# Modulation columns by block transposes and a sum along the free axis, in place of products with a column of ones

## The chip, the cores and the metric

The kernel runs on one core of one Trainium2 chip. The metric is the device time of one execution in microseconds (us). A core has a matrix engine (TensorE, PE in the profile, with its weight loads as PEld), a vector engine (VectorE, DVE), an activation engine (ScalarE, ACT), GpSimd (POOL), and a sync engine (SyncE, SP) whose queue here issues the loads from HBM. TensorE writes to PSUM, eight banks of 128 partitions x 512 fp32 numbers; the other engines read PSUM and SBUF.

## The reference

Two layers of a diffusion backbone: 256 latent tokens with 256 context tokens, 1024 features. Layer 0 is latent attention with a gated linear recurrence beside it, layer 1 a Hyena operator; each layer ends in a mixture of 16 experts. What the change touches is the modulation: a vector of 1024 conditioning features is multiplied with a 1024 x 6144 matrix per layer, and its six pieces of 1024 shift, scale or gate the activations.

```python
mod = (silu_c @ ada_w[layer] + ada_b[layer])[:, None, :]
sh1, sc1, g1, sh2, sc2, g2 = jnp.split(mod, 6, axis=-1)
h_lat = modulate(rms_norm(x, norm1_g[layer]), sh1, sc1)     # h * (1 + sc1) + sh1
...
x = x + g1 * o_lat
h_lat = modulate(rms_norm(x, norm2_g[layer]), sh2, sc2)
```

For the context tokens of layer 0 the same is done with a second conditioning vector. All is fp32.

## The kernel before

The matrix `ada_w` is used once, as a vector times a matrix, so it is streamed from HBM in tiles of 1 MB through a ring of nine buffers (the name `w`), in one fixed order of loads on SyncE's queue that the other weights share. A piece of 1024 outputs, called step (l, s), is made in two halves of 512. Pieces 0 and 1 of layer 0 are made in the prologue (`ada_first`). The later ones are made in the background of other work: `ada_step` does one of eight portions of a step each time it is called. A table (`PLAN`) says by which engine each half is made.

- A "V" half: VectorE multiplies each row of weights with its conditioning scalar and adds, lines 444 and 446. The result `e` is 128 x 512, a partial sum in each partition, and the sum over the 128 partitions is still to be made.
- A "P" half: TensorE multiplies with the conditioning columns `cs`, 32 wide, four products side by side in the four 32-column groups of the array, line 437, and ScalarE copies the result out. In `e` there are then four partial sums, in partitions 0, 32, 64 and 96, and everything between them is zero.

A step that is done ripens for a few calls (`LAG`). Then a gate piece is spread over rows (`ada_row`), and a shift or scale piece is turned into columns of 128 features by `ada_columns`: it takes the 512 numbers of a half to four columns of 128 partitions. It does this with a product: a block of 128 x 128 of `e` is the stationary operand and a column of ones (or, in the prologue, two columns of zeros and ones, `selc`, one for the latent and one for the context vector) is the moving one, so that the sum over partitions comes out with the features along the partitions. VectorE then adds the bias out of PSUM (line 377), and for a scale piece takes 1 + scale times the gain of the norm (line 379).

`ada_columns` is called 16 times: four times in the prologue (pieces 0 and 1 of layer 0, two halves, both vectors), and 12 times later in pairs, one pair for each of the steps (0,3), (0,4), (1,0), (1,1), (1,3) and (1,4). Step (0,3) has two V halves, (1,4) two P halves, the other four one of each.

What lies around the late calls: the recurrence (lines 898 to 925), the key, value and query projections (lines 953 to 1013), and attention by heads: scores (line 1078) with the row maxima on VectorE (lines 1079 and 1080) and the exponential on ScalarE (line 1081); the 128 x 128 transposes of the probabilities (line 1091); their products with the values, 64 columns wide (line 1105), scaled by VectorE (line 1108); and a transpose of these (line 1114). Then comes the output projection (`project_out`, line 512), and layer 0's experts (from line 1199 on). Tables of numbers (`SEQ`, `ATT`, `OUTB`) say how many background portions are put in at which place. Each engine works through its own queue in order. The build arranges every queue by its own estimate of when operands are there, so that rows of several lines are mixed, and a change in one function moves others.

Of the kernel before, what the change touches and what calls it, by code (L numbers as in the profile page):

```python
# [14 lines left out]
OP = mybir.AluOpType  # L15
# [46 lines left out]
PLAN = {(0, 3): "VV", (1, 2): "VV", (1, 4): "PP", (1, 5): "PP"}  # L62
# [104 lines left out]
def build(tc, A, dbg=None, stop=None):  # L167
    nc = tc.nc
    V, S, G, T = nc.vector, nc.scalar, nc.gpsimd, nc.tensor
# [18 lines left out]
    def ps():  # L188
        return pp.tile([128, 512], F32, tag="ps", name=nm("ps"))
# [138 lines left out]
    ident = kc[:, KC["ident"]:KC["ident"] + 128]  # L328
    tri = kc[:, KC["tri"]:KC["tri"] + 128]
    selrow = kc[:, KC["selrow"]:KC["selrow"] + 128]  # L330
    selc = kc[:, KC["selc"]:KC["selc"] + 2]
    iota = kc[:, KC["iota"]:KC["iota"] + CAP]
    lt = kc[:, KC["lt"]:KC["lt"] + 16]
    ones = kp.tile([128, 128], F32, name="ones")
# [30 lines left out]

    grow = {}

    def ada_columns(l, s, hf, use, e, lcol, n):
        p2 = ps()
        for m in range(4):  # L370
            T.matmul(p2[:, n * m:n * m + n], e[:, m * 128:m * 128 + 128], lcol[:, :n], start=True, stop=True)
        pv = p2[:, :4 * n].rearrange("p (m n) -> p m n", n=n)
        b = pc("adab", l * 48 + s * 8 + hf * 4, 4)
        for i in range(n):
            kind = ("c" if i else "") + ("1" if s < 3 else "2")
            o = mc(l, use + kind)[:, hf * 4:hf * 4 + 4]
            V.tensor_tensor(o, pv[:, :, i], b, op=OP.add)
            if use == "sc":
                V.scalar_tensor_tensor(o, o, 1.0, pc("n1" if s < 3 else "n2", l * 8 + hf * 4, 4),
                                       op0=OP.add, op1=OP.mult)  # L380
# [28 lines left out]
    def ada_step():  # L409
        for r in ripe:  # L410
            r[0] += 1
        if ripe and ripe[0][0] > LAG:
            l, s, use, e = ripe.pop(0)[1]
            for hf in range(2):
                if use == "row":
                    r = l * 12 + s * 2 + hf
                    V.scalar_tensor_tensor(e[hf][0:24], adab, ident[0:24, r:r + 1], e[hf][0:24], op0=OP.mult, op1=OP.add)
                    ada_row(l, s, hf, e[hf])
                else:
                    ada_columns(l, s, hf, use, e[hf], ones, 1)  # L420
        if not current:
            if not todo:
                return bool(ripe)
            e = ada_alloc[0]("e", 2, 512)
# [34 lines left out]
    def bg(n=1):  # L459
        for _ in range(n):  # L460
            ada_step()
# [300 lines left out]
    with ExitStack() as pa:  # L762
# [22 lines left out]
        for i, (src, dst) in enumerate(((ctx, ctxn), (x, y))):  # L785
            for k2 in range(4):
                p = ps()
                for k in (2 * k2, 2 * k2 + 1):
                    for t in range(2):
                        m = k % 2 * 256 + t * 128  # L790
# [42 lines left out]
        for hf in range(2):  # L833
            e = []
            for s in range(2):
                if hf and not UXL:
                    ux_sum(2 * s, 0)
                    if s == 0:
                        ux_sum(1, 0)
                e.append(ada_first(s, hf, t4))  # L840
            for s, use in enumerate(("sh", "sc")):
                ada_columns(0, s, hf, use, e[s], selc, 2)
            if hf and not UXL:
                ux_sum(3, 0)
            for k in range(4 * hf, 4 * hf + 4):
                for i, (o, kd) in enumerate(((0, "c1"), (256, "1"))):
                    v = hT[hf][:, k % 4, o:o + NT]
                    m, a = mc(0, "sc" + kd)[:, k:k + 1], mc(0, "sh" + kd)[:, k:k + 1]
                    if (2 * k + i) % 3:
                        V.tensor_scalar(v, v, m, a, op0=OP.mult, op1=OP.add)  # L850
                    else:
                        S.activation(v, v, AF.Identity, scale=m, bias=a)
# [290 lines left out]
    n = NW + N8 - 3 + NX[0]  # L1143
# [371 lines left out]
    with w0 as ws:  # L1515
# [14 lines left out]
        r = moe(0, route0, ws, filters, FJ, FILLS, turned)  # L1530
# [6 lines left out]
        p = ps()  # L1537
        for t in range(2):
            o = slice(t * 128, t * 128 + 128)
# [228 lines left out]
```

## Time and profile before

| what | us |
| --- | --- |
| median of 3 runs | 955.71 |
| lowest and highest of them | 954.07, 956.16 |
| the profiled execution's own time | 955.92 |
| its span in the trace | 954.1 |
| TensorE busy in the span | 874.8 |
| VectorE busy in the span | 458.9 |
| ScalarE busy in the span | 228.6 |

The profile comes from one execution, so durations and sums belong to its 955.92 us; the span is the part between the first and the last instruction in the trace. An engine's busy time says what share of the span it worked, not whether the end waits for it; the waits, and the timeline of the stretch, say that. In timelines, a row is a run of equal instructions: its start, its length from the first to the end of the last, the count, and in brackets how long the engine sat idle before it and what ended that. A fp32 product shows as two records, one for each of its passes; a transpose shows as one.

### The profile page before, as it was taken

The numbers are of one execution on the slowest core, as the hardware profiler recorded it, in microseconds if no ns is written. First come the engines' busy times: TensorE is split into PE (matmuls) and PEld (weight loads), VectorE is DVE, ScalarE is ACT, GpSimd is POOL, SyncE is SP. The second block draws the span as 40 slices with busy tenths as digits, with TensorE's granted clock in tenths as the row PEclk, the third lists the DMA queues.
The fourth block names the chain that finished last, engine by engine and source line by source line (L and its number), as shares of the span: only waits on it lengthen the run. The fifth ranks groups of instructions, "written<-read, shape, count | busy, mean of one in ns | idle before, by whom it ended". The sixth has DMA issues, their size and how long they took to land. (4 is left out here: it accounts for less than half of the span.)

```text
span 954.1 us, 10948 instructions
## 1 busy us (share of the span) xinstructions
PE 874.8 (92%) x4040; PEld 457.0 (48%) x4040; DVE 458.9 (48%) x1104; ACT 228.6 (24%) x446; POOL 15.7 (2%) x21
## 2 busy tenths in 40 slices
PE   3998999999989999899999599999999999988984
PEld 2444755575553543333443288677554442322421
DVE  5359775762464464445522466876172333122123
ACT  3266413440321122222211312211031110100112
POOL 0000000000000010101100000000000000000000
PEclk9999999998989999999999799999989999999997
DMA  9956679476499999999989883642289999999994
GB/s 350 344 186 242 226 242 356 159 258 221 166 371 393 369 337 387 388 397 396 393 331 347 308 276 121 242 155 89 89 298 396 390 396 387 403 390 397 397 386 151
DMA packets 130567, 289.32 MB, mean 303 GB/s; under 512 B 6828, under 2 KB 8876, under 8 KB 130500
## 3 DMA queue, kind: packets, MB, share of 16 engines
q1 hardware_dynamic: 129428, 286.39, 82.2%
q10 hardware_dynamic: 1072, 2.10, 0.7%
q8 instruction: 35, 0.57, 0.2%
q14 instruction: 32, 0.26, 0.1%
HBM read 287.42 MB, written 1.05 MB: 302 GB/s over the span
## 5 line engine op out<-in xcount | busy, mean ns | idle before, releaser
L1239 PE MATMUL ps<-w,xe 128*64 128x512 f32 (+1 forms) x696 | 173.5, 597 | 2.6 <-DMA w<-in_moe_w 2.6
L1239 PEld LDWEIGHTS ps<-w,xe 128*64 128x64 f32 (+1 forms) x696 | 49.9, 129 | 87.8 <-issue 79.1
L1267 PE MATMUL ps<-w,at 128*64 128x512 f32 (+1 forms) x344 | 86.0, 597 | 4.5 <-DMA w<-in_moe_w 2.7
L1589 PE MATMUL ps<-xt,w 128*128 128x256 f32 x384 | 87.6, 388 | 1.8 <-ACT xt L1553 1.8
L1589 PEld LDWEIGHTS ps<-xt,w 128*128 128x128 f32 x384 | 74.6, 196 | 14.4 <-ACT xt L1553 2.1
L1286 DVE TENSOR_TENSOR x<-x,ps 128x512 f32<-128x512 f32 x56 | 37.0, 684 | 62.5 <-PE ps L1284 62.5
L1273 DVE SCALAR_TENSOR_TENSOR ye<-ps,gs,grow 128x512 f32<-128x512 f32 x28 | 21.0, 748 | 85.1 <-PE ps L1267 85.1
L1239 PE MATMUL ps<-sp,xe 128*64 128x512 f32 (+1 forms) x216 | 54.8, 598 | 1.4 <-DMA sp<-in_moe_w 1.4
L446 DVE SCALAR_TENSOR_TENSOR e<-w,sg,e 128x512 f32<-128x512 f32 x70 | 51.5, 746 | 3.5 <-DMA w<-in_ada_w 2.8
L1267 PEld LDWEIGHTS ps<-w,at 128*64 128x64 f32 (+1 forms) x344 | 26.8, 130 | 50.5 <-issue 39.8
L1275 ACT ACTIVATE yeh<-ye 128x512 fp32r<-128x512 f32 x28 | 17.6, 630 | 119.6 <-DVE ye L1273 119.6
L1239 PE MATMUL ps<-x,xe 128*64 128x512 f32 (+1 forms) x112 | 37.5, 596 | 1.6 <-DMA x<-in_moe_w 1.6
L1249 DVE TENSOR_TENSOR th<-th,ps 128x512 f32<-128x512 f32 x14 | 9.6, 688 | 59.8 <-PE ps L1239 59.8
L1239 PEld LDWEIGHTS ps<-sp,xe 128*64 128x64 f32 (+1 forms) x216 | 16.0, 132 | 30.2 <-issue 26.8
L1267 PE MATMUL ps<-sp,at 128*64 128x512 f32 (+1 forms) x112 | 27.4, 599 | 3.0 <-ACT at L345 1.7
L1215 ACT ACTIVATE xe<-ps,modc 128x256 f32<-128x256 f32 (+1 forms) x32 | 15.8, 539 | 59.8 <-DVE xe L1213 59.8
L830 PE MATMUL ps<-hT,w 128*128 128x512 f32 x64 | 29.7, 623 | 0.4 <-DMA w<-in_ev_w_in 0.4
L512 PE MATMUL ps<-w,x 128*128 128x512 f32 x64 | 28.4, 595 | 0.7 <-ACT x L1603 0.7
L512 PE MATMUL ps<-w,mix 128*128 128x512 f32 x64 | 28.9, 603 | 0.0
L1244 ACT ACTIVATE th<-ps 128x512 f32<-128x512 f32 x14 | 8.4, 597 | 82.3 <-PE ps L1239 66.8
L1277 DVE TENSOR_TENSOR yel<-ye,yeh 128x512 fp32r<-128x512 f32 x28 | 19.3, 691 | 16.7 <-ACT yeh L1275 10.4
L437 PE MATMUL ps<-w,cs 128*32 128x512 f32 x160 | 27.3, 689 | 0.0
(355 smaller groups left out, 1334.2 us busy)
## 6 DMA issues: line engine op xcount, KB each, us to landing
w<-in_moe_w SPq DMA_DIRECT2D x126, 1024.0 KB, 14.0
w<-in_ada_w SPq DMA_DIRECT2D x48, 1024.0 KB, 7.2
sp<-in_moe_w SPq DMA_DIRECT2D x41, 1024.0 KB, 14.9
x<-in_moe_w SPq DMA_DIRECT2D x21, 1024.0 KB, 14.1
w<-in_od_w_in SPq DMA_DIRECT2D x12, 1024.0 KB, 8.0
w<-in_ev_w_in SPq DMA_DIRECT2D x4, 1024.0 KB, 10.9
w<-in_ev_w_out SPq DMA_DIRECT2D x4, 1024.0 KB, 7.3
w<-in_moe_w SPq DMA_DIRECT2D x8, 512.0 KB, 9.8
```

Of the source, the lines that this page charges most:

```text
L437: T.matmul(part[hf][32 * q:32 * q + 32, :], cs[:, k - 3 + q, :], get(("ada", l, s, hf, k // 4))[:, q, :], start=(k == 3), stop=(k == 7), t ...
L446: V.scalar_tensor_tensor(eh, w[hf], c, eh, op0=OP.mult, op1=OP.add)
L512: T.matmul(po[t][n], a[:, k, t * 128:t * 128 + 128], b[:, n * 512:n * 512 + 512], start=(k == korder[0] and i == 0), stop=(k == korder[-1] ...
L830: T.matmul(uxp[b], get(("wux", hf))[:, k % 4, b * 128:b * 128 + 128], hT[hf][:, k % 4, :], start=(k == 0), stop=(k == KD - 1))
L1215: S.activation(e[:, k, :w], p[:, w:2 * w], AF.Identity, scale=sc[:, k:k + 1], bias=sh[:, k:k + 1])
L1239: T.matmul(p[room * i:room * i + room, :], xe[j // 2][:, k, o:o + room], weight(nme, e, k), start=(k == 0), stop=(k == KD - 1), tile_posit ...
L1267: T.matmul(p[room * i:room * i + room, :], act[j][:, o:o + room], weight("w2", e, k, n), start=(k == 0), stop=(k == 3), tile_position=(0, ...
L1273: V.scalar_tensor_tensor(e, po[j, n], gs[j], grow[l, 5][:, n * 512:n * 512 + 512], op0=OP.mult, op1=OP.mult)
L1275: S.activation(h, e, AF.Copy)
L1277: V.tensor_tensor(o, e, h.bitcast(F32), op=OP.subtract)
L1286: V.tensor_tensor(xs, xs, p, op=OP.add)
L1589: T.matmul(pb, w[:, k % 4, b * 128:b * 128 + 128], hT[:, k, :], start=(k == 0 and b % 2 == 0), stop=(k == KD - 1 and b % 2 == 1))
```

## The change

`ada_columns` makes the four blocks into transposes (out of `e` into the four quarters of a whole PSUM bank) and lets VectorE sum along the free axis, which now holds what were the partitions. Of a V half (and of nothing else) all 128 numbers of a row are summed, 128 partitions x 4 x 128; of a P half and in the prologue only the four that are not zero, strided by 32 (`four`). The bias is then added from SBUF to SBUF. The prologue's calls make two such short sums, one for each vector. In all there are 64 transposes where there were 64 products, and 20 reductions more on VectorE: 6 full ones and 14 short ones, 8 of these in the prologue. Behind the function all line numbers are 5 higher.

```diff
--- before.py
+++ after.py
@@ -365,16 +365,21 @@
 
     grow = {}
 
-    def ada_columns(l, s, hf, use, e, lcol, n):
+    def ada_columns(l, s, hf, use, e, four, n):
+
         p2 = ps()
         for m in range(4):
-            T.matmul(p2[:, n * m:n * m + n], e[:, m * 128:m * 128 + 128], lcol[:, :n], start=True, stop=True)
-        pv = p2[:, :4 * n].rearrange("p (m n) -> p m n", n=n)
+            T.transpose(p2[:, m * 128:m * 128 + 128], e[:, m * 128:m * 128 + 128], ident)
+        pv = p2.rearrange("p (m q r) -> p m q r", m=4, q=4)
         b = pc("adab", l * 48 + s * 8 + hf * 4, 4)
         for i in range(n):
             kind = ("c" if i else "") + ("1" if s < 3 else "2")
             o = mc(l, use + kind)[:, hf * 4:hf * 4 + 4]
-            V.tensor_tensor(o, pv[:, :, i], b, op=OP.add)
+            if four:
+                V.tensor_reduce(o, pv[:, :, :, i], axis=mybir.AxisListType.X, op=OP.add)
+            else:
+                V.tensor_reduce(o, p2.rearrange("p (m r) -> p m r", m=4), axis=mybir.AxisListType.X, op=OP.add)
+            V.tensor_tensor(o, o, b, op=OP.add)
             if use == "sc":
                 V.scalar_tensor_tensor(o, o, 1.0, pc("n1" if s < 3 else "n2", l * 8 + hf * 4, 4),
                                        op0=OP.add, op1=OP.mult)
@@ -417,7 +422,7 @@
                     V.scalar_tensor_tensor(e[hf][0:24], adab, ident[0:24, r:r + 1], e[hf][0:24], op0=OP.mult, op1=OP.add)
                     ada_row(l, s, hf, e[hf])
                 else:
-                    ada_columns(l, s, hf, use, e[hf], ones, 1)
+                    ada_columns(l, s, hf, use, e[hf], PLAN.get((l, s), "VP")[hf] == "P", 1)
         if not current:
             if not todo:
                 return bool(ripe)
@@ -839,7 +844,7 @@
                         ux_sum(1, 0)
                 e.append(ada_first(s, hf, t4))
             for s, use in enumerate(("sh", "sc")):
-                ada_columns(0, s, hf, use, e[s], selc, 2)
+                ada_columns(0, s, hf, use, e[s], True, 2)
             if hf and not UXL:
                 ux_sum(3, 0)
             for k in range(4 * hf, 4 * hf + 4):
```

The order on the engines moves too. TensorE at attention, where step (1,0) becomes columns (`e_1071` before, `e_1083` after); the order of before, then that of after, in which line 372 is the transpose, 442 was 437, 1083 was 1078, 1096 was 1091 and 1119 was 1114:

```order
L371 MATMUL ps_1265<-ones,e_1071 128x1 x4
L371 MATMUL ps_1271<-ones,e_1071 128x1 x4
L437 MATMUL ps_1278<-w_1215,cs 32x512 x4
L1078 MATMUL ps_1284<-kT_948,qT_949 128x512
L1078 MATMUL ps_1289<-kT_948,qT_949 128x512
L1114 MATMUL ps_1294<-kc,o_1248 128x128 x2
L1091 MATMUL ps_1299<-kc,pm_1218 128x128 x4
L437 MATMUL ps_1278<-w_1313,cs 32x512 x2
L1091 MATMUL ps_1305<-kc,pm_1218 128x128 x4
L1078 MATMUL ps_1317<-kT_948,qT_949 128x512
L1078 MATMUL ps_1322<-kT_948,qT_949 128x512
L437 MATMUL ps_1278<-w_1313,cs 32x512 x2
```

```order
L372 MATMUL ps_1277<-kc,e_1083 128x128 x4
L372 MATMUL ps_1284<-kc,e_1083 128x128 x4
L442 MATMUL ps_1292<-w_1227,cs 32x512 x4
L1083 MATMUL ps_1298<-kT_960,qT_961 128x512
L1083 MATMUL ps_1303<-kT_960,qT_961 128x512
L442 MATMUL ps_1292<-w_1327,cs 32x512 x4
L1119 MATMUL ps_1308<-kc,o_1260 128x128 x2
L1096 MATMUL ps_1313<-kc,pm_1230 128x128 x4
L1096 MATMUL ps_1319<-kc,pm_1230 128x128 x4
L1083 MATMUL ps_1331<-kT_960,qT_961 128x512
L1083 MATMUL ps_1336<-kT_960,qT_961 128x512
```

The four packed products of the second weight tile stood two and two, around transposes and scores; now they stand together.

TensorE a little later, where step (1,1) becomes columns (`e_1204` before, `e_1216` after) between the products of the probabilities with the values (`vt` and `pt`); the order of before, then of after, in which line 1110 was 1105 and 442 was 437:

```order
L1105 MATMUL ps_1393<-vt_698,pt_1348 128x64 x2
L371 MATMUL ps_1415<-ones,e_1204 128x1 x4
L371 MATMUL ps_1422<-ones,e_1204 128x1 x3
L1105 MATMUL ps_1393<-vt_698,pt_1348 128x64 x6
L1105 MATMUL ps_1393<-vt_698,pt_1367 128x64 x8
L371 MATMUL ps_1422<-ones,e_1204 128x1
L437 MATMUL ps_1430<-w_1389,cs 32x512 x4
L437 MATMUL ps_1430<-w_1437,cs 32x512 x4
L1114 MATMUL ps_1442<-kc,o_1412 128x128 x2
```

```order
L1110 MATMUL ps_1407<-vt_708,pt_1362 128x64 x2
L372 MATMUL ps_1429<-kc,e_1216 128x128 x4
L372 MATMUL ps_1437<-kc,e_1216 128x128 x4
L442 MATMUL ps_1446<-w_1403,cs 32x512 x4
L1110 MATMUL ps_1407<-vt_708,pt_1362 128x64 x6
L1110 MATMUL ps_1407<-vt_708,pt_1381 128x64 x8
L442 MATMUL ps_1446<-w_1453,cs 32x512 x4
L1119 MATMUL ps_1458<-kc,o_1426 128x128 x2
```

The last product of the columns no longer stands behind the block of value products, and the packed products of the first weight tile moved from behind that block to ahead of it.

VectorE at the first of these places, from the columns' bias add on; before, then after, in which 381 is the full reduction, 379 the short one, 382 the bias add and 1084 was 1079:

```order
L377 TENSOR_TENSOR modc<-ps_1265,pk 128x4
L446 SCALAR_TENSOR_TENSOR e_1204<-w_1311,sg,e_1204 128x512
L377 TENSOR_TENSOR modc<-ps_1271,pk 128x4
L1079 TENSOR_REDUCE nmx<-ps_1284 128x1
L1080 TENSOR_SCALAR nmx<-nmx 128x1
L1079 TENSOR_REDUCE nmx<-ps_1289 128x1
L1080 TENSOR_SCALAR nmx<-nmx 128x1
L343 COPY pt_1298<-ps_1305 128x512
```

```order
L381 TENSOR_REDUCE modc<-ps_1277 128x4
L451 SCALAR_TENSOR_TENSOR e_1216<-w_1325,sg,e_1216 128x512
L379 TENSOR_REDUCE modc<-ps_1284 128x4
L382 TENSOR_TENSOR modc<-modc,pk 128x4
L1084 TENSOR_REDUCE nmx<-ps_1298 128x1
L382 TENSOR_TENSOR modc<-modc,pk 128x4
L1085 TENSOR_SCALAR nmx<-nmx 128x1
L1084 TENSOR_REDUCE nmx<-ps_1303 128x1
L1085 TENSOR_SCALAR nmx<-nmx 128x1
L343 COPY pt_1312<-ps_1319 128x512
```

Two reductions are new, and they and the bias adds stand ahead of the row maximum of the next scores, or between it and its scaling.

## Rows read from the trace of the kernel before

**Rows 1.** The page: the span, the engines' busy time, the granted clock by slices.
```profile
span 954.1 us, 10948 instructions
PE 874.8 (92%) x4040; PEld 457.0 (48%) x4040; DVE 458.9 (48%) x1104; ACT 228.6 (24%) x446; POOL 15.7 (2%) x21
...
PEclk9999999998989999999999799999989999999997
```

**Rows 2.** The chain that ended last, its earliest piece: start us, us, what.
```profile
542.60 0.09 issue
```

**Rows 3.** Waits of TensorE, 100 to 232 us: in total, times, longest us.
```profile
PE ps L1091 <- ACT pm L1081: 1.2, 1, 1.2
```

**Rows 4.** Waits of SyncE's load queue, 140 to 280 us, the first.
```profile
SPq L219 <- PE ps L512: 30.8, 4, 13.4
```

**Rows 5.** Instructions of line 371: ns min/median/max, first and last start, forms.
```profile
L371 PEld LDWEIGHTS ps<-ones,e x96: 188/192/334, 102.2 to 276.1; 128*128 128x128 f32 x96
L371 PE MATMUL ps<-ones,e x96: 167/251/353, 102.5 to 276.2; 128*128 128x1 f32 x96
```

**Rows 6.** Timeline at pairs A (first row) and C: start us, us.
```profile
102.23 2.00 PEld L371 LDWEIGHTS ps<-ones,e 128*128 128x128 f32 x16
...
197.60 1.86 PEld L371 LDWEIGHTS ps<-ones,e 128*128 128x128 f32 x16
...
199.48 1.07 PE L437 MATMUL ps<-w,cs 128*32 128x512 f32 x8
...
203.05 1.05 PE L437 MATMUL ps<-w,cs 128*32 128x512 f32 x4
```

**Rows 7.** Timeline around pair D, weight loads, and the products behind it.
```profile
207.32 3.65 PEld L1105 LDWEIGHTS ps<-vt,pt 128*128 128x128 f32 x32 [0.84 <-issue]
210.83 0.92 PEld L1091 LDWEIGHTS ps<-kc,pm 128*128 128x128 f32 x8
...
213.25 1.64 PEld L371 LDWEIGHTS ps<-ones,e 128*128 128x128 f32 x14
214.81 3.92 PEld L1105 LDWEIGHTS ps<-vt,pt 128*128 128x128 f32 x28
218.61 0.55 PEld L371 LDWEIGHTS ps<-ones,e 128*128 128x128 f32 x2
...
219.18 3.64 PE L437 MATMUL ps<-w,cs 128*32 128x512 f32 x16
```

**Rows 8.** Timeline at pair F, weight loads.
```profile
268.56 2.25 PEld L371 LDWEIGHTS ps<-ones,e 128*128 128x128 f32 x10
...
275.58 0.76 PEld L371 LDWEIGHTS ps<-ones,e 128*128 128x128 f32 x6
```

**Rows 9.** By windows: length, busy time of engines, granted clock, DMA share, GB/s.
```profile
211.00:212.00 1.00, 1.00 (x11) 1.00 (x11) 0.42 (x1) 0.41 (x1) 0.00 (x0) 1.00 0.91 352
...
218.00:219.00 1.00, 1.00 (x7) 1.00 (x6) 0.96 (x2) 0.00 (x0) 0.00 (x0) 0.50 0.96 365
```

**Rows 10.** VectorE's bias add and two reductions: ns min/median/max, forms.
```profile
L377 DVE TENSOR_TENSOR modc<-ps,pk x20: 150/156/163, 30.5 to 276.8; 128x4 f32<-128x4 f32 x20
...
L1079 DVE TENSOR_REDUCE nmx<-ps x16: 669/688/692, 171.3 to 206.4; 128x1 f32<-128x512 f32 x16
...
L655 DVE TENSOR_REDUCE sm<-rg x2: 186/186/186, 263.1 to 705.2; 128x8 f32<-128x32 f32 x2
```

**Rows 11.** Timeline of VectorE: idle time behind the pairs, in brackets.
```profile
120.65 1.41 DVE L954 TENSOR_SCALAR cT<-ps,pk 128x512 f32<-128x512 f32 x2 [3.55 <-PE ps L953]
...
149.57 0.69 DVE L969 TENSOR_SCALAR y<-y 128x1024 f32<-128x1024 f32 x1 [2.01 <-ACT y L968]
...
201.64 0.69 DVE L1079 TENSOR_REDUCE nmx<-ps 128x1 f32<-128x512 f32 x1 [1.74 <-PE ps L1078]
...
228.05 0.16 DVE L377 TENSOR_TENSOR modc<-ps,pk 128x4 f32<-128x4 f32 x1 [8.26 <-PE ps L371]
```

**Rows 12.** Timeline of TensorE in the prologue, behind the columns.
```profile
38.92 13.52 PE L830 MATMUL ps<-hT,w 128*128 128x512 f32 x27 [0.42 <-DMA w<-in_ev_w_in]
```

## The prediction

> **What bounds the kernel now.** I read the page first: its first line, the busy shares and the row of the granted clock [rows 1]. TensorE is busy 92% of 954.1 us, at nearly full clock in most slices, so it is the first suspect. The chain of waits cannot say more, because it reaches back only to 542.6 us [rows 2], and all twelve late calls of `ada_columns` lie earlier. So I read their own stretch, 100 to 232 us, by the list of waits of TensorE: it waited once, 1.2 us [rows 3]. There TensorE is back to back, and an instruction less on it ends the stretch earlier. What is saved also has to reach the end: from 140 to 280 us the loads' queue stood still 30.8 us in four pieces until TensorE freed a tile in line 512 [rows 4]. The weight stream waits for TensorE there and not the other way round, so it should move forward with it.
>
> A call in column form makes four products with a 128x128 stationary block and one moving column. They are fp32 and run in two passes: 12 calls left 96 records, with a median of 192 ns for the weight load and 251 ns for the product [rows 5]. These overlap; a pair of calls (two halves of a step) held the weight port 1.86 to 2.00 us with 16 records, about 0.117 us each [rows 6]. One column does not make them cheap: the weight load is the price.
>
> **TensorE, the calls themselves.** A transpose of the same block is one record instead of two. The profile has 128x128 transposes already, those of line 1091: eight take 0.92 us [rows 7], the same pace of 0.115 us. A pair after the change has eight. So each of the five pairs up to 232 us (I call them A to E: steps (0,3), (0,4), (1,0), (1,1), (1,3)) falls from 1.86 to 0.92 us: 5 x 0.94 = **4.7 us**. The upper end, by pair A's 2.00, is 0.8 us more over all five. The sixth pair, F, (1,4), lies in layer 0's experts: ten records at 268.56 us that hold 2.25 us, and six at 275.58 us that hold 0.76 [rows 8]. Eight transposes at the pace of the first ten leave 8/10 x 2.25 = 1.80, so 0.45 + 0.76 = **1.2 us**.
>
> **Order at C.** In the order of before, the products of w_1313 go two and two, with transposes and scores between; in that of after all four go together. Eight records of line 437 take 1.07 us and four take 1.05 [rows 6]: the 32-column packs cost by the pack, not by the product. One pack less saves **1.0 us**.
>
> **The clock at D.** Here the rows show something that no count of instructions gives. From 213.25 us TensorE did 14 one-column records and then 64-column ones of line 1105, and within these the granted clock fell: it was 1.00 at 211 to 212 us and 0.50 at 218 to 219 [rows 7, 9], that is 1.2 GHz in place of 2.4. An earlier run of 32 such 64-column records (207.32 us) kept the full clock; ahead of it stood no one-column products. In the new order eight transposes and one pack of four 512-column products (w_1403) stand ahead of the 64-column block. I take it that the clock then stays. What that gives: 28 records of line 1105 held 3.80 us to the next start, and at the earlier pace, 28/32 x 3.65, they need 3.19: 0.61. The two packs of line 437 took 3.64 us at 219.18 and at full clock need 2 x 1.07 [rows 6]: 1.50. The last two one-column records took 0.55 in place of 2 x 0.117: 0.32. Together **2.4 us**, and zero if the clock falls as before.
>
> The transposes of line 1091 ran between two stretches at a granted 1.00 [rows 7, 9], but they were too few to show whether they hold the clock up by themselves. The Trainium skill, "TensorE: Matmul & The Clock Gate", Part 4 on PE-mode transpose, speaks against my step: it says that for transposes the full rate does not engage and that they do not count as the engine's work in the same way. By that rule the stretch after the change would look as idle as before, and the sum would be 949.7 in place of 947.3; the trace neither confirms nor refutes it, though it shows transposes at full clock.
>
> **VectorE, what is added.** Each call gets a reduction ahead of the bias add (which stays, from SBUF and not PSUM; I price it at the 156 ns of line 377). No reduction of this shape exists before. The full one (halves summed by VectorE, 512 values per partition) is nearest to line 1079's reduction of 512 values from PSUM, 688 ns; the short one (halves made by packed products, 16 values, strided) to line 655's of 32 values, 186 ns [rows 10]. Bounds for the short one: 0.16 for a small operation, 0.69 for a full one. So A gains 2 x 0.69 = 1.38 us of VectorE, B to E 0.87 each, or up to 1.03 with one small operation's time for waiting on its own result; 4.9 to 5.5 us in all. What covers it is VectorE's idle time behind each pair: 3.55 us at 120.65 after A; after B 2.01 us at 149.57, with little before; 1.74 us at 201.64 after C; and 8.26 us at 228.05, behind D and ahead of E [rows 11]. Queued behind the reductions at C are the score maxima (now line 1084) that ScalarE's softmax and then TensorE wait for. There TensorE also arrives 0.94 + 1.0 us earlier, and the idle 1.74 shrinks to below zero by 0.2: I charge 0.2. At B I charge 0.5, the middle of 0 and 1.0. **0.7 us** is given back. If all cover were gone, the whole 5.5 would be.
>
> **The prologue.** Four calls with two moving columns become 16 transposes and 8 short reductions (1.5 us of VectorE). Behind them TensorE starts line 830 at 38.92 us only when a weight load has landed [rows 12], so an earlier end gives nothing. Nor do I charge the reductions: only those of the second half (0.75 us) stand ahead of features that are wanted after the first half's products. Without that cover they cost 0.75, which the range holds.
>
> **Sum.** 4.7 + 1.2 + 1.0 + 2.4 = 9.3, less 0.7, is 8.6 us. The profiled run took 955.92 us (span 954.1), 0.2 from the median of 955.71, so the sum is made on it: 955.92 - 8.6 = **947.3**.
>
> **Rivals.** (1) The clock at D still falls, because the columns and blocks ahead of it are still too little work, or because of the page's rule. For it: the 64-column block itself is unchanged. Against: a pack of wide products has been put ahead of it. 6.2 us of gain: 949.7. (2) VectorE takes its added time from every pair, since the shared consumers (maxima, copies out of PSUM) all come later. For it: B has no pause near. Against: the pauses of [rows 11]. 9.3 - 5.5 = 3.8 of gain: 952.1. (3) Nothing arrives at the end: from 256 us on the experts' weights come as fast as the DMA moves them, and the end is set by that stream whatever TensorE does at 200. Against: the queue's waits for TensorE in [rows 4]. 955.9. (4) Slower: VectorE, not TensorE, sets the pace between 100 and 232 us as soon as a full reduction is put ahead of its evictions; TensorE then waits and what it saved is void, the clock falls at D all the same, and only F keeps its 1.2. 955.92 + 5.5 - 1.2 = 960.2. It decides where the pause behind a pair is shorter than what is added to it (1.4 at A, 1.0 at B to E); by [rows 11] that is so at B alone.
>
> **Chances.** The forecast 0.50; the clock falls all the same 0.20; VectorE at every pair 0.12; nothing arrives 0.10; slower by VectorE 0.08. A measurement of this kernel can tell about 0.2% from no change, some 1.9 us. The first three are faster by more: 0.82; same 0.10; slower 0.08. The range leaves out the last two: its upper end is rival 2's 952.1 and half the spread of the three runs (954.07 to 956.16, so 1.0), 953.1. Its lower end is the forecast with no lateness of VectorE (0.7), pairs at A's length (0.8) and the same 1.0: 944.8.
>
> **What would show it.** Pair C should hold the weight port about 0.92 us for 8 records, and the products behind it should start nearly 1 us earlier against the scores. At D the granted clock should be 1.00 in the microseconds in which 64-column products run; if it reads 0.50 there, rival 1 holds. The full reduction should take about 0.69 us and the short one about 0.19. TensorE should wait for VectorE no more than 1 us in 100 to 232 us; a wait at each pair is rival 2, and an unmoved line 512 with all its waits is rival 4. If the experts of layer 0 begin 7 us earlier and the end does not move, it is rival 3. The forecast is wrong above all if the fall of the clock only moves to another place, since 2.4 of 8.6 us hang on it.

## The result and the profile after

The changed kernel takes 945.32 us (median of 4 runs, 944.74 to 946.41), the kernel before beside it 954.89: a ratio of 0.9912, 95% interval 0.9889 to 0.9935. Two more measurements gave 944.6 against 953.25 (0.9911, 0.9890 to 0.9931) and 945.77 against 954.67 (0.9895, 0.9877 to 0.9913). So the change gains 8.7 to 9.6 us, about 1%. The prediction was 947.3, with 944.8 to 953.1. The two profiled executions are 955.92 and 945.29 us. One execution of the kernel before took 2497.75 us and stands in no ratio of this document.

The page of the changed kernel, its lines that answer to [rows 1]:

```profile
span 943.4 us, 10841 instructions
...
PE 863.5 (92%) x3976; PEld 447.2 (47%) x3976; DVE 462.8 (49%) x1124; ACT 228.9 (24%) x446; POOL 15.7 (2%) x21
...
PEclk9999999999899999999999799999979999999998
```

TensorE is busy 11.3 us less, VectorE 3.9 us more. The new instructions by source line, as in [rows 5] and [rows 10] (min/median/max in ns; 372 is the transpose, 379 the short reduction, 381 the full one):

```profile
L372 PEld LDWEIGHTS ps<-kc,e x64: 138/141/230, 29.5 to 261.7; 128*128 128x128 f32 x64
...
L379 DVE TENSOR_REDUCE modc<-ps x14: 154/166/175, 30.4 to 262.4; 128x4 f32<-128x16 f32 x14
...
L381 DVE TENSOR_REDUCE modc<-ps x6: 680/682/692, 100.9 to 223.5; 128x4 f32<-128x512 f32 x6
```

The reductions cost about what was forecast (0.68 and 0.17 us where 0.69 and 0.19 stood), and the transposes are one record each. Pair C in the timeline of weight loads, which answers to [rows 6]:

```profile
193.19 0.91 PEld L372 LDWEIGHTS ps<-kc,e 128*128 128x128 f32 x8
```

It is 0.91 us where it was 1.86. Behind it two packs of line 442 stand, of 1.06 us each, where three packs stood. Pair D in the timeline of TensorE, which answers to [rows 7], and the granted clock right behind it, which answers to [rows 9]:

```profile
206.88 1.04 PE L372 MATMUL ps<-kc,e 128*128 128x128 f32 x8
207.85 1.06 PE L442 MATMUL ps<-w,cs 128*32 128x512 f32 x8
208.85 3.34 PE L1110 MATMUL ps<-vt,pt 128*128 128x64 f32 x28
212.12 1.06 PE L442 MATMUL ps<-w,cs 128*32 128x512 f32 x8
```

```profile
210.00:212.00 2.00, 2.00 (x20) 1.00 0.81 231
212.00:214.00 2.00, 2.00 (x14) 1.00 1.03 386
```

The 64-column block and the pack behind it run at the full clock, at the paces that the prediction took for them.

### Where the time went, place by place

The same work starts earlier after the change; how much earlier, read from the first or last start of a line's products in both traces (before, after; the difference is what was gained up to there):

| up to | before | after | earlier by |
| --- | --- | --- | --- |
| line 830, first product (prologue) | 38.9 | 38.1 | 0.8 |
| line 884, first product | 54.5 | 52.0 | 2.5 |
| line 953, first (behind pair A) | 118.6 | 115.3 | 3.3 |
| line 1013, first (behind pair B) | 150.5 | 146.0 | 4.5 |
| line 1091, last (behind pair C) | 212.8 | 206.4 | 6.4 |
| line 512, first (behind pair D) | 223.2 | 213.4 | 9.8 |
| line 512, last (behind pair E) | 254.7 | 243.5 | 11.2 |
| line 665, first (choice of experts) | 264.8 | 255.7 | 9.1 |
| line 1239, first (behind pair F) | 276.4 | 265.1 | 11.3 |
| line 1494, last of its first form | 493.9 | 480.5 | 13.4 |
| line 512 of layer 1, last | 696.8 | 683.3 | 13.5 |
| line 1199 of layer 1, first block's last | 716.1 | 705.9 | 10.2 |
| span | 954.1 | 943.4 | 10.7 |

Lines are named as in the kernel before; in the changed kernel each number is 5 higher. A to E and C's pack run about as forecast. Four entries are none of the prediction's steps: the 2.5 us of the prologue, the 2.1 lost at line 665, the 1.9 gained around line 1494, and the 3.3 lost in layer 1. The experiments take these up, with the clock at D. A "fall" of the clock is a stretch in which the granted clock is 0.50 and not 1.00; what it costs is half its length where TensorE is busy throughout.

### The profile page after: what moved, and what is told of

It is laid out like the page before. It is cut to its first block, busy times and chain, and to the rows that moved or that the text cites. A ratio compares the mean times of both kernels' runs of the same rounds, so it can differ in the third digit from the quotient of the medians.

```text
span 943.4 us, 10841 instructions
## 1 busy us (share of the span) xinstructions
PE 863.5 (92%) x3976; PEld 447.2 (47%) x3976; DVE 462.8 (49%) x1124; ACT 228.9 (24%) x446; POOL 15.7 (2%) x21
## 5 line engine op out<-in xcount | busy, mean ns | idle before, releaser
L1244 PE MATMUL ps<-sp,xe 128*64 128x512 f32 (+1 forms) x216 | 54.5, 598 | 1.4 <-DMA sp<-in_moe_w 1.2
L930 PE MATMUL ps<-w,hT 128*128 128x288 f32 (+1 forms) x96 | 26.8, 434 | 0.0
```

The source lines that it names most:

```text
L930: T.matmul(p[:, :n], hT[k // 4][:, k % 4, t * 128:t * 128 + 128], get((w, k // 4))[:, k % 4, :], start=(k == 0), stop=(k == KD - 1))
L1244: T.matmul(p[room * i:room * i + room, :], xe[j // 2][:, k, o:o + room], weight(nme, e, k), start=(k == 0), stop=(k == KD - 1), tile_posit ...
```

## The experiments

The theory that goes into them: TensorE's records are what sets the time up to 244 us, VectorE's new work is covered, the clock at D stays up because of what the new order puts into that stretch, and the differences elsewhere are falls of the clock and one moved instruction.

### 1. The same two programs again

No edit: the kernel before and the changed one, profiled a second time, since several falls of the clock stood at places that the change does not touch.

> The kernel before, unchanged, in a second profiled execution. Theory one (a fall of TensorE's clock belongs to the program): the clock falls at the same work as in the first profile, at 39, 90, 217, 268, 490, 538, 702 and 712 us, and every line starts within 0.3 us of where it did. Rival (some falls depend on when the execution began and differ between executions of one program): at least one of the falls at 39 or 490 us, where the work ahead is the same in the changed kernel and did not bring a fall there, is gone or has moved, and lines behind it start 1.7 us earlier or later.

> The changed kernel, unchanged, in a second profiled execution. Theory one: the clock is full at 206 to 224 us and falls at 248, 258, 524, 688 and 698 us as in its first profile; 945.3 us. Rival: some of these falls move, and the time of single executions differs by multiples of about 1.7 us.

Measured: the changed kernel took 944.6 us and has the same falls, none at D. The kernel before took 956.14 us in one execution and 969.91 in the profiled one, in which the granted clock was 0.95 and not 1.00 almost throughout; the times of that profile are not compared here, only the places of its falls. It fell at 39 and at D (220 to 227 us there) as in the first profile, and at 275, 544 and 722 us, but not at 90 us and not at lines 1494 and 1495, and it fell at 33 and 264 us, where it had not. So theory one is wrong for the kernel before, and the rival holds. Here are the two executions of the same program at line 1494 (490 to 498 us), each by the timeline of TensorE. The first:

```profile
489.94 1.79 PE L1494 MATMUL ps<-spec,fixed 128*128 128x512 f32 x2 [1.13 <-ACT spec L1468]
491.53 1.92 PE L1495 MATMUL ps<-spec,fixed 128*128 128x512 f32 x2
```

The second:

```profile
497.88 1.16 PE L1494 MATMUL ps<-spec,fixed 128*128 128x512 f32 x2 [1.13 <-ACT spec L1468]
498.87 1.07 PE L1495 MATMUL ps<-spec,fixed 128*128 128x512 f32 x2
```

The work ahead and the wait of 1.13 us are the same; one execution had half the clock there and the other not. So the 1.9 us that the changed kernel gained at this line are no effect of the change; in its third profile (experiment 7) the changed kernel has that fall too. The falls in the profiles of this kernel and its versions cost 1.7, 3.4, 5.1, 6.8 or 8.5 us of clock each. In the first profile before they add up to 22.2 us up to 930 us, in the profile after to 18.8: a difference of 3.4, where the two profiles are 10.7 apart. How much of the 3.4 reaches the end is not shown. Single runs of the kernel before lie between 950.5 and 956.7 us, without the two of 969.91 and 2497.75. The mean clock alone does not put them in order: one of 951.7 us had 0.967, one of 955.1 had 0.971.

### 2. The prologue alone, the later calls alone

The edit is a switch for the two forms of the columns, set by call:

```diff
-        for m in range(4):
-            T.transpose(p2[:, m * 128:m * 128 + 128], e[:, m * 128:m * 128 + 128], ident)
+        new = NEW(l, s, hf, n)
+        if not new:
+            lcol = selc if n == 2 else ones
+            for m in range(4):
+                T.matmul(p2[:, n * m:n * m + n], e[:, m * 128:m * 128 + 128], lcol[:, :n], start=True, stop=True)
...
+NEW = lambda l, s, hf, n: n == 2     # p_only; n == 1 in l_only
```

> Only the prologue's four calls in the new form, the twelve later ones as before. By the prediction's step (the prologue waits for a weight load anyway): within 0.2% of the kernel before, and line 830's counterpart starts at 38.9 us. Theory now, from the two traces: 2.5 us faster than before, 0.8 because that start was waiting for TensorE's columns and not for the load, and 1.7 because the clock does not fall at 39 us. If the fall at 39 us comes back and only the 0.8 stays, the fall is not owed to the columns.

> Only the twelve later calls in the new form, the prologue as before. Prediction: all of its 8.6 us. Theory now: by 244 us it is 8.6 us ahead of the kernel before (11.1 less the prologue's 2.5). In the expert stage of layer 1, VectorE's order is that of the kernel before here (the bias of the gate rows behind the choice of experts, not ahead of it), so the 2.85 us that TensorE waited there in the changed kernel are not lost: 9 to 12 us faster than before in all, about as fast as the changed kernel or faster. Rival (what the changed kernel won is owed to the prologue's calls): under 5 us faster.

Measured: the prologue alone 950.88 against 953.25 us, ratio 0.9978 (0.9959 to 0.9997); the later calls alone 948.19, ratio 0.9942 (0.9919 to 0.9964). The two gains, 2.4 and 5.1 us, add up to 7.4 of the 8.7 that the changed kernel gained beside them; their intervals are 0.3 to 3.9 and 3.4 to 7.7, so the part that is missing cannot be told from noise. With the later calls alone the line of 512 starts 6.7 us earlier (216.5 against 223.2) and ends 8.0 earlier, though 0.6 us were lost in the prologue to a fall at 32 us; that is the 8.6 us of the theory by that point. The end is only 7.1 earlier by its profile and 5.1 by the medians: the 9 to 12 expected are wrong, and so are the prediction's 8.6 for these calls alone. In the profile 1.7 us of it went to a longer fall, at 527 us (8.5 us of clock against 6.8 at 538 before). The prologue's columns alone give this start of line 830 (line 846 in that kernel; its products, in the timeline of TensorE):

```profile
37.59 0.90 PE L380 MATMUL ps<-kc,e 128*128 128x128 f32 x4 [0.50 <-ACT e L346]
38.33 1.88 PE L846 MATMUL ps<-hT,w 128*128 128x512 f32 x4
```

It is 0.6 us earlier than in [rows 12], although a weight load was said to hold it there. No fall at 39 us follows, and line 884 is 2.4 us earlier. At D, where the old form stands, the clock falls and costs 5.1 us here.

### 3. Pair D back in the old form

```diff
-NEW = lambda l, s, hf, n: n == 2
+NEW = lambda l, s, hf, n: (l, s) != (1, 1)
```

> The changed kernel with pair D alone, step (1,1), in the old form (one-column products in the old order around it). Theory (the one-column records and the missing pack ahead of the 64-column block bring the fall): the granted clock is 0.50 again within the 64-column block and the packs behind it, and line 517's counterpart of line 512 starts 3 to 3.5 us later than in the changed kernel (2.4 to 3.4 from the clock, 0.94 from the pair). VectorE's order in layer 1's expert stage is that of before here, so TensorE's wait of 2.85 us there is gone, and the total is within 1 us of the changed kernel's. Rival (the fall depends only on when the stretch begins): the clock stays at 1.00 at D, and only 0.9 us is lost there.

Measured: 947.59 us against 954.48, ratio 0.9936 (0.9918 to 0.9954). The old order of TensorE is back there, and so is the fall. The timeline of its weight loads (376 is the one-column product, 1121 the 64-column one):

```profile
207.03 1.64 PEld L376 LDWEIGHTS ps<-ones,e 128*128 128x128 f32 x14
208.59 4.65 PEld L1121 LDWEIGHTS ps<-vt,pt 128*128 128x128 f32 x28
```

and a window behind it, with the granted clock ahead of the last two columns:

```profile
213.00:216.00 3.00, 3.00 (x17) 1.26 (x20) 1.23 (x4) 0.00 (x0) 0.00 (x0) 0.50 0.41 160
```

The line of 512 starts at 217.4, 4.0 us later than in the changed kernel: somewhat more than the 3 to 3.5 expected. The total is 1.5 us longer by profile (span 945.0 against 943.4), not within 1. Over all profiles of the whole kernel's versions the fall at D is there in 4 of 4 with pair D in the old form (before, its repeat, the prologue alone, this one), and in 0 of 7 with the new form. The rival, that only the moment decides, does not fit this place.

### 4. What holds the clock

A train of unused TensorE work at the start of the changed kernel, in long blocks first:

```diff
+        cold(192)                # transposes
+        for _ in range(2):
+            wide(48)
+            transposes(128)
+            wide(48)
+            one_column(64)
+            wide(48)
+            columns64(64)
```

> The changed kernel with a train of extra TensorE work put in at the start, whose results are not used: 192 transposes of 128x128 from a cold start; then, twice, 48 products of 512 columns followed by 128 transposes, by 64 one-column products (128 records) or by 64 products of 64 columns (128 records); then the sequence of pair D, four times each as before (64-column, transposes, one-column, 64-column), with the one-column products replaced by transposes, and with a wide product added. Theory: one-column and 64-column products back to back lose the full clock within their 15 us, and the D-like sequence falls more often with one-column products than with transposes and a wide product. On transposes: by the rows of before they hold the full clock while they run, so it should stay at 1.00 over 128 of them. By the Trainium skill, TensorE: Matmul & The Clock Gate, Part 4, transposes do not count as the engine's work, and the clock should fall within them and not rise in the first 192.

Measured in one execution: the three blocks of 128 records, timeline of TensorE (350 transposes, 354 one-column products, 358 products of 64 columns):

```profile
77.35 14.14 PE L350 MATMUL ps<-kc,x 128*128 128x128 f32 x128
...
132.52 22.55 PE L354 MATMUL ps<-ones,x 128*128 128x1 f32 x128
...
197.84 14.40 PE L358 MATMUL ps<-ones,x 128*128 128x64 f32 x128
```

and the windows in them, with busy time of TensorE, granted clock, DMA share and GB/s:

```profile
77.00:91.00 14.00, 14.00 (x128) 1.00 0.01 1
...
140.00:155.00 15.00, 15.00 (x72) 0.50 0.00 1
...
198.00:212.00 14.00, 14.00 (x129) 1.00 0.01 1
```

The second round is alike (14.14, 24.29 and 14.40 us). All three keep TensorE busy all the time. The clock stayed at 1.00 through the transposes and the 64-column products and fell to 0.50 within the one-column products, and what follows them pays too: the 48 wide products behind took 43.07 and 42.96 us, behind the other blocks 41.37 to 41.42. So the theory's half on 64-column products is wrong. The 192 transposes from the cold start are the other half of the question: they started 0.21 us apart at first and 0.11 us apart from 18 us on, so the clock rose with nothing but transposes on TensorE. The Trainium skill's sentence that transposes do not count ("TensorE: Matmul & The Clock Gate", Part 4) is not borne out by this case: the clock rose within the first 192 of them, and 128 later ones ran 14.14 us at a granted 1.00. The D-like sequences in this run fell in 1 of 4 with one-column products and in none of the other 8, too few to tell; so they were run alone, with their middles exchanged:

```diff
+        def around(n, middle):
+            wide(n)
+            columns64(16)
+            transposes(18)
+            columns64(2)
+            middle()
+            columns64(14)
...
+        for n in range(24, 36):
+            around(n, lambda: one_column(8))
+            around(n, lambda: transposes(8))
+            around(n, both)      # one_column(8), then wide(2)
```

> The changed kernel with another train of unused TensorE work at the start: the surroundings of pair D (16 products of 64 columns, 18 transposes, 2 products of 64 columns, a middle, 14 products of 64 columns), each behind 24 to 35 wide products, 12 times with each of three middles: 8 one-column products; 8 transposes; 8 one-column products and 2 wide ones. Theory (one-column records are what does not hold the clock, transposes do): falls in several of the 12 with one-column products, in none with transposes; with the wide products added fewer than with one-column products alone. Rival (the wide pack that the new order put ahead of the 64-column block holds the clock, and the form of the columns does not matter): as many falls with transposes as with one-column products, none with the wide ones.

One turn of it, timeline of TensorE (346 transposes, 350 one-column, 354 64-column, 342 wide):

```profile
81.68 1.90 PE L350 MATMUL ps<-ones,x 128*128 128x1 f32 x16
83.44 5.74 PE L354 MATMUL ps<-ones,x 128*128 128x64 f32 x28
...
118.12 1.04 PE L346 MATMUL ps<-kc,x 128*128 128x128 f32 x8
119.00 3.24 PE L354 MATMUL ps<-ones,x 128*128 128x64 f32 x28
...
148.61 1.90 PE L350 MATMUL ps<-ones,x 128*128 128x1 f32 x16
150.37 1.96 PE L342 MATMUL ps<-x,kc 128*128 128x512 f32 x4
152.17 3.23 PE L354 MATMUL ps<-ones,x 128*128 128x64 f32 x28
```

Over the 12 turns the clock fell in 11 behind one-column products, in 0 behind transposes, and in 0 behind one-column products with two wide ones. So transposes in place of the one-column products are enough by themselves, and the rival (only the pack counts) is out. Wide products behind the one-column ones are enough too, but those of the train are two products with stationary blocks of 128 columns, 1.96 us together; the kernel's pack at D (line 442) is four products with blocks of 32 columns, 1.06 us together. Whether that pack alone would have held the clock was not run, so what each half of the change did at D in the kernel stays open.

### 5. The new work of VectorE, twice

```diff
                 V.tensor_reduce(o, p2.rearrange("p (m r) -> p m r", m=4), axis=mybir.AxisListType.X, op=OP.add)
+                V.tensor_reduce(o, p2.rearrange("p (m r) -> p m r", m=4), axis=mybir.AxisListType.X, op=OP.add)
```

> The changed kernel with each of the six full reductions of VectorE done twice, 6 x 0.69 = 4.1 us more on VectorE, 1.4 at pair A and 0.7 at B to E. Theory (VectorE's pauses behind the pairs cover it, the prediction's charge for lateness was 0.7 us for the first reduction): at most 1.4 us later at 244 us than the changed kernel, no wait of TensorE for a VectorE result over 1 us between 100 and 232 us. Rival (2) of the prediction (VectorE takes its time from every pair): 4.1 us later.

Measured: 945.06 us, ratio 0.9909 (0.9878 to 0.9939), as the changed kernel. Line 512's last product starts at 243.4 us, in the changed kernel at 243.5. TensorE's waits from 95 to 225 us are one line, as in [rows 3]:

```profile
PE ps L1097 <- ACT pm L1087: 1.2, 1, 1.2
```

4.1 us more on VectorE cost nothing, at no pair: no line of the table above, up to line 512's last, starts later than in the changed kernel. (In the changed kernel the weight port waited twice for VectorE's new rows, 0.8 us each time, once of them at D; TensorE's products ran on without a gap.) The charge of 0.7 us for lateness was too high, and rivals (2) and (4) are out.

### 6. The moved bias rows of layer 1

In the changed kernel layer 1 lost 3.3 us between lines 512 and 1199. VectorE and ScalarE in that stretch, and TensorE behind them (658, 660 and 663 are steps of the choice of experts, 663 its last; 422 adds the bias to a gate row, of step (1,5), and waits for ScalarE's copy of the packed products, 446):

```profile
691.47 0.19 DVE L658 TENSOR_TENSOR rg<-rg 128x32 f32<-128x32 f32 x1
693.13 0.60 ACT L446 ACTIVATE e<-ps 128x512 f32<-128x512 f32 x1 [2.37 <-PE ps L442]
693.76 0.74 DVE L422 SCALAR_TENSOR_TENSOR e<-fixed,kc,e 24x512 f32<-24x512 f32 x1 [2.10 <-ACT e L446]
...
694.42 0.17 DVE L660 TENSOR_REDUCE sm<-rg 128x8 f32<-128x32 f32 x1
...
696.36 0.19 DVE L663 TENSOR_TENSOR rg<-rg,sm 128x32 f32<-128x32 f32 x1
...
696.70 0.37 PE L670 MATMUL ps<-rg,kc 128*128 128x16 f32 x2 [2.85 <-DVE rg L663]
```

The build has put 422 ahead of 660, where before its counterpart (417) stood behind the choice's last step (line 658 of before, 663 of after); the kernel before, timeline of VectorE:

```profile
706.48 0.19 DVE L658 TENSOR_TENSOR rg<-rg,sm 128x32 f32<-128x32 f32 x1
...
707.92 0.73 DVE L417 SCALAR_TENSOR_TENSOR e<-fixed,kc,e 24x512 f32<-24x512 f32 x1
```

In the changed kernel VectorE stands 2.10 us with the whole choice queued behind, and TensorE then 2.85. No step of the change is within 400 us of it; the order moved all the same. Not all of the 3.3 us is that wait: falls of the clock in this stretch cost 5.1 us in the changed kernel and 3.4 before. With the old order of VectorE and 5.1 us of falls, in the versions of experiments 3 and 2 (prologue alone), the stretch took 20.2 us; before it took 19.3, in the changed kernel 22.6. So about 2.4 of the 3.3 are the order. The edit fixes these rows behind the choice:

```diff
         route.count()
+        if l:
+            bg_all()
         place(0, route.pos, firsts)
```

> The changed kernel with one thing moved: in layer 1 the two bias rows of the gate step (line 422) and its row products (line 391) are issued right behind the experts' count, ahead of the one-hot places, in a fixed order, so that they cannot stand ahead of the router's choice on VectorE. Theory (in the changed kernel VectorE waited 2.1 us for ScalarE's copy with the whole choice queued behind, and TensorE 2.85 us for the choice): that wait goes, the row products fill TensorE's wait for the places, and the kernel is 2.5 to 5 us faster than the changed one, 940 to 943 us. Rival (that stage is hidden under the weight stream of layer 1's experts): within 1 us of the changed kernel.

Measured: 943.85 us, ratio 0.9887 (0.9865 to 0.9910) beside 0.9912 of the changed kernel; by these intervals the two cannot be told apart. The wait is gone and the row products stand where they were meant to (391, timeline of TensorE in this kernel):

```profile
698.33 1.98 PE L391 MATMUL ps<-e,ones 128*128 128x512 f32 x4 [1.19 <-DVE e L422]
699.76 2.47 PE L1204 MATMUL ps<-P,yh 128*128 128x256 f32 x16
```

The stretch from line 512 to line 1199 takes 16.6 us here, 6.1 less than in the changed kernel, but 3.4 of that are falls of the clock (1.7 us of cost against 5.1); and this execution came to it 2.1 us later than the changed kernel's, most of it from a fall at 39 us. On balance the first stage of layer 1's experts is 3.0 us earlier than in the changed kernel: its transposes of line 1259 start 3.0 us earlier at 724, 755 and 781 us, and 3.1 at 816, but 0.6 at 856 and 0.2 at 919. In between TensorE waits for weights; in this kernel, then in the changed one, again the timeline of TensorE:

```profile
814.45 3.66 PE L1272 MATMUL ps<-sp,at 128*32 128x512 f32 x12 [0.73 <-ACT at L345]
818.73 4.54 PE L1272 MATMUL ps<-sp,at 128*32 128x512 f32 x24 [0.62 <-DMA sp<-in_moe_w]
823.86 1.90 PE L1272 MATMUL ps<-sp,at 128*32 128x512 f32 x4 [0.59 <-DMA sp<-in_moe_w]
```

```profile
817.52 6.30 PE L1272 MATMUL ps<-sp,at 128*32 128x512 f32 x36 [0.73 <-ACT at L345]
824.41 1.90 PE L1272 MATMUL ps<-sp,at 128*32 128x512 f32 x4 [0.58 <-DMA sp<-in_moe_w]
```

The block begins 3.1 us earlier, and its last four records start 0.6 us earlier: in both kernels they wait for a load. The DMA engines were busy without a pause in both, at 386 to 403 GB/s from 760 to 880 us. So the theory is right about the wait, which was real and is gone, and wrong about the end: the 940 to 943 us were not reached, and most of the lead went into the weight stream of layer 1's experts, as rival (3) of the prediction had it for layer 0's. What the wait cost the changed kernel at the end is not established: the medians are 1.5 us apart (943.85 and 945.32, not measured side by side).

### 7. Pair F ahead of the gather, and the changed kernel a third time

```diff
         place(0, route.pos, firsts)
+        if not l:
+            bg_all()
```

> The version with layer 1's gate rows put behind the count, and in layer 0 pair F's eight transposes put ahead of the experts' gather, where TensorE waits 1.5 us for the places. Theory: F's 0.9 to 1.7 us go into that wait, so 0.5 to 1.5 us faster than the version with the gate rows alone. Rival (the weight stream of layer 0's experts or a fall of the clock takes it): within 0.5 us of that version.

> The changed kernel once more, on the chip and in the rounds of the last version, for their comparison. Falls of the clock at D: none, as in its first two profiles. 944 to 946 us.

Measured: 943.93 us, ratio 0.9881 (0.9865 to 0.9898), and beside it the changed kernel 945.77 (0.9895, 0.9877 to 0.9913), whose profile has no fall at D. That profile is of the slowest of its four executions, 949.32 us, outside the 944 to 946 expected. It has falls that the first two do not have, one of them at line 1494 (1499 in the changed kernel):

```profile
479.65 2.06 PE L1499 MATMUL ps<-spec,fixed 128*128 128x512 f32 x2 [1.14 <-ACT spec L1473]
```

and it lacks the one at 248 us, so that its line 665 starts 2.0 us earlier than in the first profile and its line 1494 is done 3.1 us later. All its falls up to 930 us cost 18.8 us, as in the first profile, and yet its span is 947.4 us against 943.4; the other 4 us are not explained. The step from the version with the gate rows alone (943.85, not measured beside it) to this one is not told apart from none, as the rival had it. In the traces the theory holds in its place: from line 665 to line 1239 this version takes 7.5 us and the one before it 9.2, with no fall in either stretch. But its fall at 250 us cost 3.4 us and not 1.7, line 665 started 1.8 us later for it, and the two are level again at line 1239 (265.2 and 265.1 us). Both versions beat the kernel before by 1.1 to 1.2%, and the changed kernel by an amount, 0.1 to 0.2%, that these runs do not establish.

## Why the prediction came out as it did

**What bounds it: right.** TensorE's back-to-back records between 100 and 232 us set the pace, and what was taken off them arrived. Doubling VectorE's new work moved nothing.

**The calls: right.** 4.7 us for A to E were forecast. By the table A gave 0.8 and B 1.2; C with its pack 1.9, where 0.94 + 1.0 stood in the sum; the 0.3 too much at B is not explained. E gave 1.4, 0.94 for the pair and the rest the tail of the old fall, which reached 0.8 us into line 512 and which the sum had left out.

**The clock at D: right, and a little larger.** 2.4 + 0.94 stood in the sum, 3.4 were gained up to line 512's start, some 0.4 more behind. The reason given was that the clock falls in the block of 64 columns behind one-column records, and stays with transposes and a pack ahead. The trains of experiment 4 show it for the transposes, and show that 64-column products alone keep the clock too; for the pack alone it is not shown. Rival (1) is out with 0 of 7 profiles.

**VectorE's lateness: the term was too large.** 0.7 us were charged, nothing was found. The idle time of [rows 11] covered the pairs, and where little stood near, at B, it needed none. What failed is taking the middle between 0 and 1.0 at B for want of a pause close by; the trace of before shows no wait of TensorE for the eviction of the columns between 100 and 232 us [rows 3].

**The prologue: the step was wrong.** It was set to zero because [rows 12] name a weight load as what TensorE waited for last. That wait was 0.42 us, and the columns ahead of it had become shorter by more, but the load also came earlier: the start moved by 0.6 to 0.8 us with a wait of 0.36 still behind it. In all eight profiles with transposes in the prologue line 830 starts at 37.8 to 38.4 us, in the three with products at 38.9, 39.4 (at a clock of 0.95) and 39.5 (behind a fall at 32 us), so the earlier load seems to go with the change; why was not tested. The other 1.7 us are the fall of the clock at 39 us, which is gone in the changed kernel. It is there in 3 of 3 profiles with two-column products in the prologue, and in 2 of 8 with transposes (both in the versions of experiments 6 and 7); that it hangs on the columns' form alone is not so, and what else decides was not shown.

**Pair F: right in itself, but the clock around it moved.** 1.2 us were forecast. The pair held the weight port 2.25 and 0.76 us before [rows 8]; after, by the timeline of weight loads, it is one row:

```profile
260.26 1.59 PEld L372 LDWEIGHTS ps<-kc,e 128*128 128x128 f32 x8
```

From line 665 to line 1239 2.2 were gained: the pair, and a fall that cost 1.7 us where the old one cost 3.4. Ahead of it a new fall at 248 us took 2.1 us back. Between 254 and 276 us next to nothing was gained, for a reason that the sum did not have. A fall between lines 512 and 665 is there in 6 of 7 profiles with the new form at D and in 1 of 4 with the old one; what brings it was not tested.

**The sum.** 8.6 us were forecast and 8.7 to 9.6 measured, while the two profiles are 10.6 apart. Up to 276 us, without the prologue, the trace has gained 8.8 us: 8.7 from A to E, and 0.1 from F with the new fall. The sum had 7.4 for A to E with 0.7 taken off for lateness, and 1.2 for F: one part came out 1.3 higher and the other 1.1 lower. The prologue's 2.5, the 1.9 around line 1494 and the loss of 3.3 in layer 1 were not in the sum, and they cancel but for about 1 us. Run alone, the later calls, which are the whole of the sum, gained 5.1 us at the end (3.4 to 7.7), and the prologue, which the sum has at zero, 2.4. So the mechanism was right where the prediction looked, and the agreement of 8.6 with 8.7 to 9.6 is owed in part to luck. The range's lower end has a slip of 0.1: five pairs at A's length are 5 x 0.14 = 0.7 us more, not 0.8. Rival (3), "nothing arrives", is wrong for what is gained before 250 us, and right for most of what the version of experiment 6 gained at 690 us.

**What was missed.** That the build's order of VectorE would change in layer 1. The prediction read the order at the places of the change alone; the difference of the two orders over the whole program shows line 422 ahead of line 660.

## What to carry to other kernels

A fp32 product with one moving column cost its weight load, twice (0.117 us a record here), and behind 16 such records the clock fell in 11 of 12 turns. A block transpose and a sum along the free axis take half the records, and a VectorE with idle time takes the sum. Where a stretch of narrow products stands between wide ones, look at the granted clock behind it before counting records, and read the changed order over the whole program, not only where the code was changed. A gain has to be followed to the next stage that waits for its loads: a lead of three microseconds at the start of layer 1's experts was 0.6 us 130 us later.

## What the runs showed that was not expected

- 128 transposes of 128x128 in a row ran at a granted 1.00 (0.110 us each), and so did 128 records of 64 columns (0.112 us each), while 128 records of one column fell to 0.50 and took 22.55 and 24.29 us. Transposes alone also brought the clock up from a cold start.
- Two wide products (1.96 us) behind 16 one-column records were enough in 12 of 12 turns to keep the 64-column block behind them at full clock; without them it fell in 11 of 12.
- The same program, with the same work and the same wait ahead, had half the clock at line 1494 in one execution and not in another. Single executions of the kernel before spread over 950.5 to 956.7 us; that the falls are the reason is likely but not shown, since an execution with the same 18.8 us of falls as another was 4 us longer.
